# Hybrid decoder trunk on one core: scores of the first query block over its own keys alone, and the last two weight blocks of w_out taken together

## The chip, the cores and the metric

The kernel runs on one core of one Trainium2 chip. The metric is the time of one execution on the device in microseconds. The times are those of whole executions; the span of a profile runs from the first to the last instruction.

## What is computed

The reference is a decoder trunk of two layers over 512 tokens of width 1024. Each layer is cut here to what matters:

```python
h = rmsnorm(x, norm_mix)
z = h @ w_in                      # q, k, v of attention; q, k, v, gates of the mLSTM; branch gates
# branch A: attention of 128-query blocks over their own and the previous block
qb = q.reshape(B, nb, 128, 2, 4, 64)
prev = jnp.pad(tb, ((0, 0), (1, 0), (0, 0), (0, 0), (0, 0)))[:, :-1]   # block 0: zeros
scores = jnp.einsum('bnqhgd,bnkhd->bnhgqk', qb, kb) * 64 ** -0.5
valid = (kpos >= 0) & (kpos <= qpos) & (qpos - kpos < 128)
scores = jnp.where(valid, scores, -jnp.inf)                # softmax with a learned sink per head
# branch B: a chunkwise mLSTM
mixed = sigmoid(g_a) * (att @ w_att_branch) + sigmoid(g_m) * (hm @ w_m_branch)
x = x + mixed @ w_out
u = relu(rmsnorm(x, norm_ffn) @ w_ff1)
x = x + (u * u) @ w_ff2           # width 4096
```

For the first query block the previous block does not exist: its scores are masked whatever they are.

## The kernel before

All matrix products run in a split form: each float32 operand is written as a high part and a low rest, and three matmuls (high by high, low by high, high by low; the function `mm3`, recorded at L45) stand for one. A dense product goes through `group_steps`: four PSUM tiles of 128x512 take their sums side by side, one weight block (`chunk`) after the other. A block is loaded by DMA from SP's queue, its high part `wh` is made on ScalarE (L190) and its low part `wl` on VectorE (L191); `wh` and `wl` have four buffers, the raw block three. A step is one block by one tile, three matmuls. At the end of a group, `finish` empties the four tiles (`evac`). The PSUM tiles come in pairs of two banks from `banks()`, and three such pairs and two auxiliary tiles (`aux`) exist.

The input projection, the output projection and the MLP are such groups. `weave` runs the list of steps of a dense group and drops small steps of the attention and of the mLSTM between them: `k_tr(b)` transposes the keys of a block into `kT` (L505 and following: ScalarE L512 and L513, VectorE L514 and L515), `q_tr(b)` transposes queries (L534, L535), `att_scores(b, kv, hp)` multiplies queries and keys for two heads into one `aux` tile, `att_softmax(b, kv)` works on four heads at once (maximum L561 and L562, exponentials L567, the sink's L569, the sum and its reciprocal L570 and L571, product L572), and the gates of the mLSTM (L620 to L633) share the same engines. The order in which each engine gets its instructions is set by a tile scheduler that works from this program and from estimated durations; each engine then runs its list strictly in that order and waits where an operand is not there.

`kT` holds five blocks of 128 keys, a block of zeros ahead of the four real ones, so that every query block reads 256 columns: its own keys and the block before. The scores of a block end on VectorE in L554, a copy under the causal mask, which also releases the `aux` tile. For the blocks after the first, the previous keys' half is copied on ScalarE (L553); for block 0 that half is filled with a large negative number by GpSimd.

The output projection runs in two halves of 512 columns, j = 0 and 1, each with eight weight blocks. The adds of its result into the residual stream (L792) are `ev_x`. After it comes the MLP: its first matrix is loaded in pieces `f` (L856), its second in pieces `raw` (L924), both from SP's queue in program order, and both are split on ScalarE (L817) and VectorE (L818). The normalised input of the MLP is transposed on TensorE (L49), copied on ScalarE (L203) and VectorE (L204); the sums for the norm are taken at L283 and L311.

Of the kernel before, what the change touches and what calls it, by code (L numbers as in the profile page):

```python
# [16 lines left out]
P = 128  # L17
T = 512
# [15 lines left out]
def hybrid_kernel(ctx, tc, x, norm_mix, w_in, att_q_norm, att_k_norm, att_sinks, m_gate_bias,  # L34
# [3 lines left out]
    ve, sc, gp = nc.vector, nc.scalar, nc.gpsimd  # L38
# [21 lines left out]
    def nm(s):  # L60
        uid[0] += 1
        return f"{s}_{uid[0]}"
# [11 lines left out]
    def temp(dt=F32):  # L74
        return now["tmp"].tile([P, T], dt, tag="t", name=nm("t"))
# [3 lines left out]
    def banks(which=None):  # L79

        if which is None:
            which = "xyf"[turn_of[0] % 3]
            turn_of[0] += 1
        return psum.tile([P, 2, T], F32, tag=which, name=nm("mm"))

    def aux(shape=(P, T)):
        return paux.tile(list(shape), F32, tag="aux", name=nm("aux"))
# [4 lines left out]
    def f32(ap):  # L92
        return ap.bitcast(F32)
# [70 lines left out]
    def chunk(src, width=T):  # L164

        with tc.high_priority():
            raw = now["wraw"].tile([P, T], F32, tag="w", name=nm("w"))
            off = 0
            for s in src:
                n = s.shape[1]  # L170
                if first_loads:

                    n0 = {0: 0, 1: 2, 2: 4, 3: 6}.get(chunks[0], 7)
                    with tc.issue_after(first_loads[n0].ins):
                        nc.sync.dma_start(raw[:, off:off + n], s)
                    chunks[0] += 1
                    if chunks[0] == 8:
                        first_loads.clear()
                else:
                    nc.sync.dma_start(raw[:, off:off + n], s)  # L180
                off += n
            wh = now["wsp"].tile([P, T], F32R, tag="wh", name=nm("wh"))
            wl = now["wsp"].tile([P, T], F32R, tag="wl", name=nm("wl"))
            n = chunks[0] - 1 if first_loads else 2
            with ExitStack() as order:
                if n < 2:

                    order.enter_context(tc.issue_after(norm0.hi[n].ins))
                    order.enter_context(tc.issue_after(norm0.lo[n].ins))
                sc.activation(wh[:, :off], raw[:, :off], AF.Copy)  # L190
                ve.tensor_tensor(wl[:, :off], raw[:, :off], f32(wh[:, :off]), op=ALU.subtract)  # L191
        return wh, wl
# [14 lines left out]
    def mm3(ps, sh, sl, mh, ml, first, last, **kw):  # L207
        pe.matmul(ps, sh, mh, start=first, stop=False, **kw)
        pe.matmul(ps, sh, ml, start=False, stop=False, **kw)
        pe.matmul(ps, sl, mh, start=False, stop=last, **kw)  # L210

    def group_steps(acts, srcs, evac, width, mm, order=None):


        order = order or list(range(len(acts)))
        ps, w = [], []

        def step(k, m):
            if k == order[0] and m % 2 == 0:
                two = banks()  # L220
                ps.extend([two[:, 0, :], two[:, 1, :]])
            if m == 0:
                w[:] = chunk(srcs(k))
            mm(ps[m], slice(m * P, (m + 1) * P), w, acts[k], k == order[0], k == order[-1])

        def finish():
            with tc.high_priority():
                for m in range(4):
                    evac(m, ps[m][:, :width])

        return [(0.25, lambda k=k, m=m: step(k, m)) for k in order for m in range(4)] + [(0, finish)]

    def feat_steps(acts, srcs, evac):

        def mm(ps, c, w, a, first, last):
            mm3(ps, w[0][:, c], w[1][:, c], a[0], a[1], first, last)

        return group_steps(acts, srcs, evac, T, mm)

    def tok_steps(acts, srcs, evac, width=T, order=None):  # L240

        def mm(ps, c, w, a, first, last):
            mm3(ps[:, :width], a[0][:, c], a[1][:, c], w[0][:, :width], w[1][:, :width], first, last)

        return group_steps(acts, srcs, evac, width, mm, order)

    def weave(fill, side=()):

        side = sorted(side, key=lambda e: e[0])
        at = 0.0  # L250
        for width, f in fill:
            while side and side[0][0] <= at + 1e-6:
                side.pop(0)[1]()
            f()
            at += width
        for _, f in side:
            f()
# [97 lines left out]
    def mixer(l, norm, late, order, phase):  # L355
# [11 lines left out]
        acts = norm.acts  # L367
# [8 lines left out]
        def ev_kv(b, ps):  # L376
            sc.activation(kvi[:, b, :], ps, AF.Copy, scale=norm.col[:, b:b + 1])

        weave(tok_steps(acts, wcols(C_Q, 512), ev_q, order=order)
              + tok_steps(acts, lambda k: [W[k * P:(k + 1) * P, C_K:C_K + 256],  # L380
                                           W[k * P:(k + 1) * P, C_IF:C_IF + 8]], ev_kv, width=264),
              late + [(6.9, norm.columns), (10.0, lambda: row.append(norm.along()))])
# [89 lines left out]

        kT = mid.tile([P, 2, HKV, (NB + 1) * P], F32R, tag="mid10", name=nm("kT"))
        kTh, kTl = kT[:, 0], kT[:, 1]
        ve.memset(f32(kT[:, :, :, 0:P]), 0.0)

        v2 = mid.tile([P, NB, HKV, 2, HD], F32R, tag="mid4", name=nm("v2"))
        v4 = kvi[:, :, 128:256].rearrange("p b (h d) -> p b h d", d=HD)
# [59 lines left out]
        def att_scores(b, kv, hp):  # L538
            if hp == 0:
                sps[b, kv] = temp()  # L540
            ps = aux()
            for i in range(2):
                c = 2 * hp + i
                lhs = qT[b, kv][:, c * P:(c + 1) * P]
                o = ps[:, i * 2 * P:(i + 1) * 2 * P]
                pe.matmul(o, lhs, kTh[:, kv, b * P:(b + 2) * P], start=True, stop=False)
                pe.matmul(o, lhs, kTl[:, kv, b * P:(b + 2) * P], start=False, stop=True)
            p4 = ps.rearrange("p (h w k) -> p h w k", h=2, w=2)
            dst = sps[b, kv][:, hp * 2 * P:(hp + 1) * 2 * P].rearrange("p (h k) -> p h k", h=2)
            if b == 0:  # L550
                gp.memset(dst, NEG)
            else:
                sc.activation(dst, p4[:, :, 0, :], AF.Copy)  # L553
            ve.copy_predicated(dst, tri_i.unsqueeze(1).to_broadcast([P, 2, P]), p4[:, :, 1, :])  # L554
# [117 lines left out]
        for i, (b, kv) in enumerate(units):  # L672
            at = 7 + 1.65 * i
            side += [(at, lambda b=b, kv=kv: att_scores(b, kv, 0)),
                     (at + 1.25, lambda b=b, kv=kv: att_scores(b, kv, 1)),
                     (at + 1.25, lambda b=b, kv=kv: att_softmax(b, kv)),
                     (at + 3.45, lambda b=b, kv=kv: att_probs(b, kv)),
                     (at + 3.45 + 2.2, lambda b=b, kv=kv: att_out(b, kv))]
            if kv == 0 and b + 1 < NB:
                if b + 2 < NB:  # L680
                    side += [(at + 1, lambda b=b: k_vec(b + 2)), (at + 1, lambda b=b: q_vec(b + 2))]
                side += [(at + 2 * 1.65 - 1.25, lambda b=b: k_tr(b + 1)), (at + 2 * 1.65 - 1.75, lambda b=b: q_tr(b + 1))]
# [84 lines left out]
        def head_tr(f):  # L767
            ps = aux()
            for b in range(NB):
                pe.transpose(ps[:, b * P:(b + 1) * P], hm[b][:, f * P:(f + 1) * P], ident)  # L770
            hmT.append(split(ps, g_head(l, f)))

        side += [(57.75 + 1.25 * f, lambda f=f: head_tr(f)) for f in range(MH)]
        weave(feat_steps(acts, wcols(C_QM, 512), ev_qk) + s0 + s1 + tok_steps(acts, wcols(C_VM, 512), ev_v)
              + a_steps(0, g0) + a_steps(1, g1) + s2 + tok_steps(acts, wcols(C_OM, 512), ev_o) + s3, side)
        sgm = [g2, g3]
        mixed = [None] * KT
# [11 lines left out]
        for j in range(2):  # L789
            def ev_x(b, ps, j=j):  # L790
                xb = xtok[b // 2][j][:, b % 2, :]
                ve.tensor_tensor(xb, xb, ps, op=ALU.add)  # L792

            weave(tok_steps(mixed, lambda k, j=j: [w_out[l, k * P:(k + 1) * P, T * j:T * (j + 1)]], ev_x),
                  norm.steps(0, 1.5, 0.5) if j else [])
        return norm

# [228 lines left out]
    order = None  # L1026
    for l in range(DEPTH):
        with ExitStack() as phase:
            norm = mixer(l, norm, late, order, phase)
        late = norm.steps(1, 1.5, 0.5)  # L1030
        with ExitStack() as phase:
            norm = mlp(l, norm, late, phase)
        late = norm.steps(0, 1.5, 0.5) if norm else []
        order = [4, 5, 6, 7, 0, 1, 2, 3]
# [40 lines left out]
```

## Time and profile before

| | |
|---|---|
| times of three runs | 1333.98, 1333.02, 1332.83 us; median 1333.02 |
| profiled execution | 1333.96 us, span 1332.2 us |
| instructions | 16887 |
| TensorE (PE) | busy 98% of the span, 6106 matmuls |
| VectorE (DVE), ScalarE (ACT), GpSimd (POOL) | 70%, 50%, 8% |
| granted clock of TensorE | 1.000 |
| HBM | read 121.84 MB, written 2.10 MB, 93 GB/s over the span |

A row of the timeline has the start, the duration, the engine, the line, the operation, the tiles (output, then inputs), the shape and the count, and in brackets the idle time before it and what ended that. Where rows are grouped, the duration spans all of them. A matmul's end is modelled, so its price in a stream is the distance between starts. Layer 1 takes about the first half of the span and layer 2 the second.

### The profile page before, as it was taken

To read this page: it belongs to the slowest core of one execution; us is meant where nothing else is said; L and a number is where in the kernel's file an instruction comes from. 1 tells how busy PE (TensorE), PEld (TensorE's weight loads), DVE (VectorE), ACT (ScalarE), POOL (GpSimd) and SP (SyncE) were. 2 spreads that over 40 slices of the span, in tenths; PEclk is the share of its full clock that TensorE was granted. 3 is DMA by queue.
4 is the path that set the end of the run, shared out by engine and by line. 5 is a ranking of instruction groups with operands and counts; after the bars stand their busy time and mean duration, and the time that the engine had idled before them with its cause. 6 is when DMAs were issued, how large, how long until landed. Compare 5 with 4: busy or idle time off the path is not lost.

```text
span 1332.2 us, 16887 instructions
## 1 busy us (share of the span) xinstructions
PE 1311.5 (98%) x6106; PEld 1078.1 (81%) x6106; DVE 927.7 (70%) x1411; ACT 666.6 (50%) x1201; POOL 107.3 (8%) x215
## 2 busy tenths in 40 slices
PE   8999999999999999999999999999999999999998
PEld 6877788888788888888888777888887888888886
DVE  4689764473576876868947887654646778678687
ACT  5468765444434344343554787554334444344343
POOL 4512300000000000000015113000000000000000
PEclk9999999999999999999999999999999999999999
DMA  5322123421523243131024221243225232332211
GB/s 151 108 77 67 64 71 87 128 96 63 195 90 127 65 131 121 64 124 44 31 66 121 69 72 64 72 127 96 95 75 186 79 127 86 121 95 95 95 48 63
DMA packets 87282, 125.02 MB, mean 94 GB/s; under 512 B 8216, under 2 KB 45184, under 8 KB 87200
## 3 DMA queue, kind: packets, MB, share of 16 engines
q1 hardware_dynamic: 86240, 123.30, 29.5%
q8 instruction: 48, 0.79, 0.2%
q10 hardware_dynamic: 576, 0.53, 0.1%
q0 software_dynamic: 384, 0.13, 0.1%
q14 instruction: 34, 0.28, 0.1%
HBM read 121.84 MB, written 2.10 MB: 93 GB/s over the span
## 4 chain that ended last, share of the span: by engine, by line
PE 88%; DVE 6%; ACT 3%; issue 1%; DMA 1%; POOL 0%; ACTq 0%; SPq 0%; DVEq 0%; POOLq 0%
PE mm L45 82%; PE aux L45 4%; PE aux L49 2%; DVE wl L191 1%; ACT t L567 1%; ACT wh L190 1%; DVE t L554 1%; DMA w<-in_w_in_dram 0%; DVE t L604 0%; ACT wh L817 0%; DMA f<-in_w_ff_dram 0%; DVE t L201 0%; DVE t L535 0%; DVE wl L818 0%; ACT junk L283 0%
## 5 line engine op out<-in xcount | busy, mean ns | idle before, releaser
L45 PE MATMUL mm<-i,wh 128*128 128x512 f32 x1664 | 521.8, 393 | 2.3 <-DVE a L654 1.1
L45 PEld LDWEIGHTS mm<-i,wh 128*128 128x128 f32 x1664 | 307.4, 188 | 65.9 <-DVE a L654 2.0
L45 PE MATMUL mm<-i,wl 128*128 128x512 f32 x832 | 324.8, 390 | 0.0
L191 DVE TENSOR_TENSOR wl<-w,wh 128x512 fp32r<-128x512 f32 (+1 forms) x208 | 140.8, 678 | 125.8 <-ACT wh L190 120.6
L190 ACT ACTIVATE wh<-w 128x512 fp32r<-128x512 f32 (+1 forms) x208 | 127.2, 612 | 145.4 <-PE mm L45 122.5
L817 ACT ACTIVATE wh<-raw 128x1024 fp32r<-128x1024 f32 x112 | 118.2, 1055 | 151.9 <-PE mm L45 116.4
L45 PEld LDWEIGHTS mm<-i,wl 128*128 128x128 f32 x832 | 156.2, 188 | 33.2 <-issue 0.5
L45 PE MATMUL mm<-wh,uh 128*128 128x512 f32 x448 | 174.5, 389 | 0.0
L45 PE MATMUL mm<-wh,ul 128*128 128x512 f32 x448 | 174.3, 389 | 0.0
L45 PE MATMUL mm<-wl,uh 128*128 128x512 f32 x448 | 174.3, 389 | 0.0
L818 DVE TENSOR_TENSOR wl<-raw,wh 128x1024 fp32r<-128x1024 f32 x112 | 136.0, 1220 | 37.8 <-ACT wh L817 37.4
L45 PE MATMUL mm<-wh,i 128*128 128x512 f32 (+1 forms) x512 | 149.7, 370 | 0.4 <-ACT wh L190 0.4
L817 ACT ACTIVATE wh<-f 128x1024 fp32r<-128x1024 f32 x64 | 67.2, 1056 | 117.6 <-PE mm L45 87.9
L45 PEld LDWEIGHTS mm<-wh,i 128*128 128x128 f32 x512 | 92.4, 189 | 15.9 <-ACT wh L190 0.8
L45 PEld LDWEIGHTS mm<-wh,ul 128*128 128x128 f32 x448 | 84.1, 188 | 17.5
L45 PEld LDWEIGHTS mm<-wl,uh 128*128 128x128 f32 x448 | 84.1, 188 | 17.5
L45 PEld LDWEIGHTS mm<-wh,uh 128*128 128x128 f32 x448 | 84.1, 188 | 17.3
L818 DVE TENSOR_TENSOR wl<-f,wh 128x1024 fp32r<-128x1024 f32 x64 | 77.7, 1221 | 29.0 <-ACT wh L817 28.9
L45 PE MATMUL mm<-wl,i 128*128 128x512 f32 (+1 forms) x256 | 94.2, 368 | 0.0
L871 DVE SCALAR_TENSOR_TENSOR u<-mm,t 128x1024 f32<-128x1024 f32 x32 | 39.1, 1222 | 69.1 <-PE mm L45 69.1
L841 DVE TENSOR_TENSOR x<-x,mm 128x1024 f32<-128x1024 f32 x64 | 77.3, 1218 | 13.6 <-PE mm L45 13.6
L45 PE MATMUL mm<-wh,a 128*128 128x512 f32 x256 | 81.4, 393 | 0.0
(215 smaller groups left out, 1621.7 us busy)
## 6 DMA issues: line engine op xcount, KB each, us to landing
w<-in_w_in_dram SPq DMA_DIRECT2D x128, 256.0 KB, 2.6
f<-in_w_ff_dram SPq DMA_DIRECT2D x64, 512.0 KB, 3.7
raw<-in_w_ff_dram SPq DMA_DIRECT2D x64, 512.0 KB, 3.4
w<-in_w_out_dram SPq DMA_DIRECT2D x32, 256.0 KB, 2.5
w<-in_w_att_branch_dram SPq DMA_DIRECT2D x16, 256.0 KB, 2.5
w<-in_w_m_branch_dram SPq DMA_DIRECT2D x16, 256.0 KB, 2.5
w<-in_w_in_dram SPq DMA_DIRECT2D x16, 128.0 KB, 2.1
out_dram<-x SPq DMA_DIRECT2D x8, 256.0 KB, 2.2
```

The source lines that it names most:

```text
L45: return nc.tensor.matmul(*args, **kw)
L49: return nc.tensor.transpose(*args)
L190: sc.activation(wh[:, :off], raw[:, :off], AF.Copy)
L191: ve.tensor_tensor(wl[:, :off], raw[:, :off], f32(wh[:, :off]), op=ALU.subtract)
L554: ve.copy_predicated(dst, tri_i.unsqueeze(1).to_broadcast([P, 2, P]), p4[:, :, 1, :])
L567: sc.activation(s3[:, i, :], s3[:, i, :], AF.Exp, bias=m[:, i:i + 1], accum_out=den[:, i:i + 1])
L817: sc.activation(hi, r, AF.Copy)
L818: ve.tensor_tensor(lo, r, f32(hi), op=ALU.subtract)
L841: ve.tensor_tensor(xh, xh, ps, op=ALU.add)
L871: ve.scalar_tensor_tensor(dst, self.ps, 0.0, rowf[0].unsqueeze(1).to_broadcast([P, 2, T]), op0=ALU.max, op1=ALU.mult)
```

## The change

Two edits are made. In `att_scores`, block 0 multiplies its queries with its own 128 keys alone, into the right half of each 256 columns of the `aux` tile; the left half is neither written nor read. With this the zero block of `kT` is read by nobody, and the memset of it goes. In the second half of the output projection (j = 1), the steps of the last two weight blocks are ordered by tile: tile 0 with block 6, tile 0 with block 7, tile 1 with block 6, and so on, in place of block 6 for all tiles and then block 7. For this `w` becomes a dictionary by block.

```diff
-    def group_steps(acts, srcs, evac, width, mm, order=None):
+    def group_steps(acts, srcs, evac, width, mm, order=None, end_pair=False):
         order = order or list(range(len(acts)))
-        ps, w = [], []
+        n = len(order) - 2 if end_pair else len(order)
+        blocks = [[k] for k in order[:n]] + ([order[n:]] if end_pair else [])
+        ps, w = [], {}
 
         def step(k, m):
 ...
             if m == 0:
-                w[:] = chunk(srcs(k))
-            mm(ps[m], slice(m * P, (m + 1) * P), w, acts[k], k == order[0], k == order[-1])
+                w[k] = chunk(srcs(k))
+            mm(ps[m], slice(m * P, (m + 1) * P), w[k], acts[k], k == order[0], k == order[-1])
 ...
-        return [(0.25, lambda k=k, m=m: step(k, m)) for k in order for m in range(4)] + [(0, finish)]
+        return ([(0.25, lambda k=k, m=m: step(k, m)) for ks in blocks for m in range(4) for k in ks]
+                + [(0, finish)])
 ...
-        ve.memset(f32(kT[:, :, :, 0:P]), 0.0)
 ...
-                pe.matmul(o, lhs, kTh[:, kv, b * P:(b + 2) * P], start=True, stop=False)
-                pe.matmul(o, lhs, kTl[:, kv, b * P:(b + 2) * P], start=False, stop=True)
+                ks = slice(b * P, (b + 2) * P)
+                if b == 0:
+                    o, ks = o[:, P:], slice(P, 2 * P)
+                pe.matmul(o, lhs, kTh[:, kv, ks], start=True, stop=False)
+                pe.matmul(o, lhs, kTl[:, kv, ks], start=False, stop=True)
 ...
-            weave(tok_steps(mixed, lambda k, j=j: [w_out[l, k * P:(k + 1) * P, T * j:T * (j + 1)]], ev_x),
+            weave(tok_steps(mixed, lambda k, j=j: [w_out[l, k * P:(k + 1) * P, T * j:T * (j + 1)]], ev_x,
+                            end_pair=j == 1),
                   norm.steps(0, 1.5, 0.5) if j else [])
```

More of the change, by code (lines that the diff above doesn't have):

```diff
@@ L238, in feat_steps, with tok_steps @@
         return group_steps(acts, srcs, evac, T, mm)
-    def tok_steps(acts, srcs, evac, width=T, order=None):
+    def tok_steps(acts, srcs, evac, width=T, order=None, end_pair=False):
         def mm(ps, c, w, a, first, last):
             mm3(ps[:, :width], a[0][:, c], a[1][:, c], w[0][:, :width], w[1][:, :width], first, last)
-        return group_steps(acts, srcs, evac, width, mm, order)
+        return group_steps(acts, srcs, evac, width, mm, order, end_pair)
     def weave(fill, side=()):
```

## The prediction

> **What bounds the kernel now.** I read the page first, then TensorE's waits, then the timeline at the edited places.
>
> ```profile
> span 1332.2 us, 16887 instructions
> ...
> PE 1311.5 (98%) x6106; PEld 1078.1 (81%) x6106; DVE 927.7 (70%) x1411; ACT 666.6 (50%) x1201; POOL 107.3 (8%) x215
> ...
> PE 88%; DVE 6%; ACT 3%; issue 1%; DMA 1%; POOL 0%; ACTq 0%; SPq 0%; DVEq 0%; POOLq 0%
> ...
> PE aux L49 <- DVE t L554: 2.2, 6, 0.4
> ...
> PE aux L49 <- DVE x L792: 0.7, 2, 0.3
> PE mm L45 <- DVE x L792: 0.5, 2, 0.2
> ```
>
> TensorE is busy for 98% of the span; only 20.7 us of 1332.2 are not its own. So a matmul that goes is worth its issue time, and a wait that TensorE gains is paid in full, if nothing later swallows either. The last three rows (engine, line, what was waited for: us in total, times, longest) are the waits beside the two edits: on L554, the masked copy that empties a PSUM tile of scores, and on L792, the adds that end w_out.
>
> The sum is made against the profiled execution, 1333.96 us, of which 1332.2 are the span and 1.76 lie around it. It stands 0.94 above the median of the three runs, 1333.02, to which the difference is added.
>
> **Part 1, the scores of block 0.** Per layer, four groups of four score matmuls (kv 0 and 1, two halves each) go from 256 columns to 128: 16 matmuls, 32 in all. Their price now, and the nearest rows for 128 columns:
>
> ```profile
> 71.59 0.64 PE L45 MATMUL aux<-kT,t 128*128 128x256 f32 x4
> 72.06 0.40 PE L45 MATMUL mm<-i,wh 128*128 128x512 f32 x1
> ...
> 73.46 0.60 PE L49 MATMUL aux<-ident,a 128*128 128x128 f32 x4
> ...
> 187.11 0.33 PE L45 MATMUL aux<-a,a 128*128 128x128 f32 x2
> 187.28 0.68 PE L45 MATMUL mm<-a,wh 128*128 128x512 f32 x2
> ...
> L49 PE MATMUL aux<-ident,a x64: 270/272/303, 62.1 to 921.6; 128*128 128x128 f32 x64
> ```
>
> A group of 256 columns takes 72.06 - 71.59 = 0.47 us, 0.118 a matmul. Two of 128 columns take 187.28 - 187.11 = 0.17, so four take 0.34: that is the row of the same kind, and I take it. Transposes of 128 columns bound it from above: four span 0.60, one lasts 0.272, so they start (0.60 - 0.272) / 3 = 0.109 apart, 0.44 a group. Half of the present price, 0.235, bounds it from below. The saving is 0.13 a group (0.03 to 0.235), over 8 groups 1.04 us (0.24 to 1.9).
>
> That TensorE's price has a floor in the load of the 128 weight columns is a rule of the Trainium skill, page "TensorE: Matmul & The Clock Gate", section "LDWEIGHTS (loading the stationary operand)": P / 1.2 ns, 107 ns for 128 columns, with no term for the moving side. The transposes' 109 ns agree with it, the pair's 85 ns does not; by it the saving would be an estimated 8 x 4 x (118 - 107) ns = 0.35 us.
>
> **The memset** is one per layer on VectorE:
>
> ```profile
> L475 DVE MEMSET kT<- x2: 485/485/485, 1.0 to 671.6; 128x512 f32 x2
> ```
>
> It stands in the first microsecond of the program and at 671.6, before the keys exist. VectorE is idle for 30% of the span there and elsewhere, and the list of who waited for the memset is empty: 0 us. If it did delay something, at most 2 x 0.485 = 1 us would be gained.
>
> **What part 1 moves.** The order in which the program stands is rebuilt with shorter scores, and it comes out otherwise at one place, alike in both layers. On ScalarE, the split `wh` (L190, at 75.09) that stood before the four exponentials of the first softmax now stands after the second of them; and the split at 80.77, ahead of the two key copies L512 and L513, now stands between them. On TensorE the transpose of the second key block (`aux<-ident,kvi`) comes one dense matmul earlier, with the last use of a weight chunk behind it. On VectorE the small step of the maximum (L562) now stands behind a gate product (L633, 0.69) instead of a rotary product (L535, 0.48). The rest of VectorE's order at this place stays, as do the queues of SP and POOL. These are the rows of that place:
>
> ```profile
> 73.81 0.73 PE L45 MATMUL aux<-kT,t 128*128 128x256 f32 x4
> ...
> 74.72 0.48 DVE L535 SCALAR_TENSOR_TENSOR t<-aux,gc,t 64x256 fp32r<-64x256 f32 x1
> ...
> 75.09 0.63 ACT L190 ACTIVATE wh<-w 128x512 fp32r<-128x512 f32 x1 [0.52 <-PE mm L45]
> ...
> 75.22 0.17 DVE L562 SCALAR_TENSOR_TENSOR m<-m,nsinks 128x4 f32<-128x4 f32 x1
> ...
> 75.42 0.69 DVE L633 TENSOR_TENSOR a<-a,a 64x512 fp32r<-64x512 f32 x1
> ...
> 75.62 0.39 ACT L567 ACTIVATE t<-t,m 128x128 f32<-128x128 f32 x1
> ...
> 77.16 0.19 ACT L569 ACTIVATE es<-es 128x4 f32<-128x4 f32 x1
> ...
> 77.39 0.16 DVE L570 TENSOR_TENSOR den<-den,es 128x4 f32<-128x4 f32 x1 [0.48 <-ACT es L569]
> ...
> 77.79 0.69 DVE L572 TENSOR_TENSOR t<-t,den 128x512 f32<-128x512 f32 x1
> ...
> 80.27 0.44 DVE L554 COPY_PREDICATED t<-tri_l,aux 128x256 f32<-128x256 int32 x1
> ...
> 80.77 0.63 ACT L190 ACTIVATE wh<-w 128x512 fp32r<-128x512 f32 x1
> ...
> 80.86 0.30 PE L49 MATMUL aux<-ident,kvi 128*128 128x128 f32 x1 [0.42 <-DVE t L554]
> 80.91 0.47 PE L45 MATMUL mm<-i,wl 128*128 128x512 f32 x1
> ...
> 81.48 0.69 DVE L191 TENSOR_TENSOR wl<-w,wh 128x512 fp32r<-128x512 f32 x1 [0.22 <-ACT wh L190]
> ...
> 82.93 0.22 DVE L515 CAST kT<-kT 64x128 fp32r<-64x128 f32 x1
> ...
> 83.10 0.73 PE L45 MATMUL aux<-kT,t 128*128 128x256 f32 x4
> ...
> 739.53 0.30 PE L49 MATMUL aux<-ident,kvi 128*128 128x128 f32 x1 [0.43 <-DVE t L554]
> ```
>
> There are two auxiliary PSUM tiles. The third score group (73.81) holds one until L554 empties it at 80.27, because the whole softmax stands before that copy on VectorE. The key transpose needs that tile, and TensorE stands idle 0.42 us for it.
>
> Now the same chain in the new order. L562 is done at 75.22 + 0.17 + (0.69 - 0.48) = 75.60, and the exponentials start at about 75.65. Four of them take 77.16 - 75.62 = 1.54, the split among them 75.62 - 75.09 = 0.53: L569 starts at 77.72 in place of 77.16, 0.56 later. VectorE waits for L569 already (0.48 at 77.39), so L570, L572, the rotary products and L554, which follow almost without a gap, all come 0.56 later, and the transpose starts at 80.86 + 0.56 = 81.42. TensorE arrives there earlier than before, by the shorter groups and by the dense matmul that now comes later. All that it has saved in three groups it spends waiting.
>
> Second step. The split that began at 80.77, before the transpose, must now wait for the last use of the weight chunk, which stands behind it: 81.42 + 0.05 (the 80.86 and 80.91 rows) + 0.47 = 81.94, 1.17 later. Its `wl` on VectorE (81.48) stands ahead of L514 and L515, as before, so L515 ends 1.17 later than 82.93 + 0.22 = 83.15. The group at 83.10, the scores of block 1, reads what L515 writes. So TensorE is 1.17 late there, the fourth group's saving spent too, and up to 1.4 if the dense matmul that it still has to do (0.23) is counted. If L562 comes no later than it did, both are 0.21 less, 0.96 and 1.19. I take 1.25 a layer, **+2.5 us** in all (1.9 to 2.8). The 739.53 row shows layer 2 with the same wait. I see no later wait on something independent of TensorE's own progress that would swallow it.
>
> **Part 2, the end of w_out.** The last 24 matmuls of the second half are the same 24, taken tile by tile. They cost nothing new; the tiles' ends move.
>
> ```profile
> 334.52 3.62 SPq L924 DMA_DIRECT2D raw<-in_w_ff_dram  x3
> ...
> 335.89 2.66 DVE L792 TENSOR_TENSOR x<-x,mm 128x512 f32<-128x512 f32 x4 [8.14 <-PE mm L45]
> ...
> 336.37 0.39 PE L45 MATMUL mm<-wh,a 128*128 128x512 f32 x1
> ...
> 336.82 0.40 PE L45 MATMUL mm<-wh,a 128*128 128x512 f32 x1
> ...
> 338.00 0.44 PE L49 MATMUL aux<-ident,x 128*128 128x128 f32 x2 [0.34 <-DVE x L792]
> ...
> 337.00:340.00 3.00, 2.41 (x14) 1.65 (x13) 2.91 (x5) 0.45 (x1) 0.00 (x0) 1.00 0.59 203
> ...
> 348.93 1.05 ACT L817 ACTIVATE wh<-f 128x1024 fp32r<-128x1024 f32 x1
> ...
> 357.60 1.10 PE L45 MATMUL aux<-t,ones 128*128 128x512 f32 x2 [0.20 <-DVE t L311]
> ...
> 1007.02 0.69 ACT L203 ACTIVATE i<-aux,gcol 128x512 fp32r<-128x512 f32 x1 [1.14 <-PE aux L49]
> ```
>
> The adds wait by pairs of tiles. Those of the second pair wait for the last matmul of all (336.82 + 0.40 = 337.22) in both orders, and the third and fourth of the four 0.66 us adds set when the transposes at 338.00 and the MLP's first matmuls start. The first two come earlier, but VectorE had finished them by 335.89 + 2 x 0.66 = 337.2 anyhow. So the two L792 waits stay: 0. If they all went, 0.7 + 0.5 = 1.2 us would be gained; if one add were later, 2 x 0.66 lost.
>
> The price is in the loads. The first `raw` load of the MLP's second matrix is issued at 334.52, when the seventh weight block is released, twelve matmuls from the end. Now that block is used until three before the end; nine matmuls at (336.82 - 336.37) / 2 = 0.225 make this load 2.0 later. The next two keep their release (the eighth block's last use). Behind them on SP's queue stand the `f` loads. In 337 to 340 the DMA engines were busy for 0.59 of the time at 203 GB/s (the last two columns), so (1 - 0.59) x 3 = 1.23 us of slack takes that up and the stream is about 0.8 late. ScalarE's L817 at 348.93 starts on its `f` as soon as ScalarE is free; its load may have landed well before or just then: the split is 0 to 0.8 late, the norm behind it on ScalarE too, and the wait at 357.60 for that norm grows by as much. I take the middle, **+0.4 us**, in layer 1. In layer 2 ScalarE is idle for 1.14 us just before the same split (1007.02, the split follows at once), so its chain is not full there: 0 (up to 0.8).
>
> **Sum.** 2.5 + 0.4 = 2.9: 1333.96 + 2.9 = 1336.9 for a profiled execution like this one, 1333.02 + 2.9 = **1335.9 us** for the median. Of the 1.04 us of matmul time saved, none is seen.
>
> **Rivals.**
>
> B, the other side: the waits do not grow. If ScalarE's and VectorE's chains have more slack than I read, or TensorE's later waits shrink by what it lost, the shorter scores remain: 1333.02 - 1.04 = 1332.0. For it: TensorE is the bound, and what it does not issue is gained. Against: the 0.42 wait exists already, so anything put into the chain ahead of L554 is paid at once. It decides where L569 comes no later than now, for which the 0.53 of the split has to find a gap among the exponentials; the rows from 75.62 on show none.
>
> C, the weight load sets the price of a short matmul, as the transposes' 0.109 has it: with B's waits the saving is 8 x 4 x (0.118 - 0.109) = 0.3 us, 1332.7. For it are the 64 transposes; against it is the pair at 187.11. This is the rule of the Trainium skill named above.
>
> D, the MLP's weights become the bound: if the stream is late by a whole 0.5 MB load, at 203 GB/s 2.6 us, in place of 0.8, layer 1 loses 2.6 - 0.4 = 2.2 more than I count: 1338.1. It decides from where the delay at L817 passes the 0.8.
>
> E, the edit of the end of w_out brings the MLP forward, the L792 waits go: 1.2 off the forecast, 1334.7. For it is only that two of four tiles end earlier; against it, that the last pair decides.
>
> **How the numbers follow.** The forecast has 0.52, B 0.25, C 0.08, D 0.09, E 0.06. The range is 1331.9 to 1337.4: down to B; up to 2.8 for the attention and 1.6 for loads late by 0.8 in both layers. Left out are about half of B, whose saving may be up to 1.9, and most of D. About 0.2% (2.7 us) is what a measurement of this kernel tells from no change: beyond it on the fast side lies only B's end with E's, 0.06; beyond it on the slow side lie the upper part of the forecast, 0.35, and D, 0.09: 0.44; within it 0.50.
>
> **What would show it.** Right: score groups of block 0 that take about 0.34; the wait at the second key transpose grown from 0.42 to about 1.6 in both layers, L554 still its releaser, with TensorE some 1.2 later at the scores of block 1; the two L792 waits unchanged; the wait for L311 near 0.6 in layer 1. Wrong: L569 no later than before; that transpose starting no later; TensorE at the end of the attention part ahead of before.

## The result, and the profile after

The changed kernel takes 1337.28 us (median of eight runs, 1336.27 to 1338.82); the kernel before, run beside it, 1333.64 (eight runs, 1332.83 to 1333.98). The ratio is 1.0028, with a 95% interval of 1.0020 to 1.0037: slower by about 3.6 us. Forecast were 1335.9, in a range of 1331.9 to 1337.4.

The page of the profile after, and TensorE's waits (engine, line, what was waited for: us in total, times, longest). Lines after the edited places are shifted: L554 is now L561, L792 is L799, L311 is L315, L569 is L576, L514 and L515 are L517 and L518.

```profile
span 1335.6 us, 16885 instructions
...
PE 1312.4 (98%) x6106; PEld 1078.1 (81%) x6106; DVE 926.3 (69%) x1409; ACT 666.4 (50%) x1201; POOL 106.7 (8%) x215
```

```profile
PE aux L49 <- DVE t L561: 3.8, 6, 1.2
...
PE aux L45 <- DVE t L561: 1.0, 2, 0.5
...
PE aux L49 <- DVE x L799: 0.7, 2, 0.3
...
PE mm L45 <- DVE x L799: 0.5, 2, 0.3
```

The span is 3.4 us longer. TensorE's busy time has not fallen. The wait for the mask copy has grown from 2.2 to 3.8 us, a new wait on the same line, for the copy of another score group, has appeared with 1.0, and the two waits on the adds at the end of w_out are what they were: 0.7 and 0.5.

The timeline after, at the place where the prediction put the loss:

```profile
71.94 0.56 PE L45 MATMUL aux<-kT,t 128*128 128x128 f32 x4
...
76.76 0.62 ACT L190 ACTIVATE wh<-w 128x512 fp32r<-128x512 f32 x1
...
78.06 0.19 ACT L576 ACTIVATE es<-es 128x4 f32<-128x4 f32 x1
...
81.16 0.44 DVE L561 COPY_PREDICATED t<-tri_l,aux 128x256 f32<-128x256 int32 x1
...
81.75 0.30 PE L49 MATMUL aux<-ident,kvi 128*128 128x128 f32 x1 [1.24 <-DVE t L561]
...
82.36 0.63 ACT L190 ACTIVATE wh<-w 128x512 fp32r<-128x512 f32 x1
...
83.03 0.69 DVE L191 TENSOR_TENSOR wl<-w,wh 128x512 fp32r<-128x512 f32 x1 [0.87 <-ACT wh L190]
...
84.02 0.42 DVE L561 COPY_PREDICATED t<-tri_l,aux 128x256 f32<-128x256 int32 x1
...
84.47 0.22 DVE L518 CAST kT<-kT 64x128 fp32r<-64x128 f32 x1
...
84.59 0.78 PE L45 MATMUL aux<-kT,t 128*128 128x256 f32 x4 [0.48 <-DVE t L561]
...
741.90 0.30 PE L49 MATMUL aux<-ident,kvi 128*128 128x128 f32 x1 [1.24 <-DVE t L561]
```

This execution was 0.35 us late already at the second score group (71.94 against 71.59): about half of that it brings from its first 50 us, and the rest it loses at the start of the first score group (68.01 against 67.62). Why is open. Without the 0.35, the sink's exponential is 0.55 later than before, the mask copy and the transpose 0.54, the end of the keys' low part 1.19, and the scores of block 1 start 1.14 later. The wait at the transpose is 1.24 in place of 0.42, in both layers, and a second wait of 0.48 stands at the scores of block 1.

### The profile page after: what moved, and what is told of

It reads as the page before. It is cut to its first block, busy times and chain, and to the rows that moved or that the text cites. A ratio compares the mean times of both kernels' runs of the same rounds, so it can differ in the third digit from the quotient of the medians.

```text
span 1335.6 us, 16885 instructions
## 1 busy us (share of the span) xinstructions
PE 1312.4 (98%) x6106; PEld 1078.1 (81%) x6106; DVE 926.3 (69%) x1409; ACT 666.4 (50%) x1201; POOL 106.7 (8%) x215
## 4 chain that ended last, share of the span: by engine, by line
PE 88%; DVE 6%; ACT 4%; issue 1%; DMA 1%; POOL 0%; ACTq 0%; SPq 0%; DVEq 0%; POOLq 0%
PE mm L45 82%; PE aux L45 4%; PE aux L49 2%; ACT t L574 1%; DVE wl L191 1%; ACT wh L190 1%; DVE t L561 1%; DVE t L611 0%; DMA w<-in_w_in_dram 0%; DVE t L201 0%; ACT wh L825 0%; DVE t L538 0%; ACT junk L287 0%; DVE t L579 0%; DMA grow<-in_norm_mix_dram 0%
```

## The experiments

Two traces with the same matmuls can be compared matmul by matmul: the start of the k-th one in this trace less its start in the trace of before is how late TensorE is there. What that grows by in a stretch is what the stretch costs, whatever came earlier. The stretches are attention 1 (63.7 to 131.3 us of before), MLP 1 (338.0 to 519.8) and attention 2 (711.2 to 795.8). In the table, "old" is the order of before and "new" that of the changed kernel; medians are in us, and each ratio is against the runs of before on the same chip (median 1333.64 for the changed kernel, 1334.06 to 1334.37 for the others). low_half has a single run and no ratio. Each stretch is that of one profiled execution. The diffs below show the lines that matter, in short form.

| kernel | order | block 0, columns | end of w_out | median | ratio (95%) | attention 1 | MLP 1 | attention 2 |
|---|---|---|---|---|---|---|---|---|
| changed kernel | new | 128 | by tile | 1337.28 | 1.0028 (1.0020 to 1.0037) | +1.77 | -0.01 | +1.51 |
| part2_only | old | 256 | by tile | 1333.69 | 0.9999 (0.9990 to 1.0007) | +0.05 | +0.36 | +0.11 |
| part1_only | new | 128 | as before | 1337.18 | 1.0024 (1.0015 to 1.0033) | +1.70 | +0.01 | +1.75 |
| old_order_short | old | 128 | by tile | 1333.95 | 1.0001 (0.9992 to 1.0010) | -0.05 | +0.45 | -0.04 |
| new_order_full | new | 256 | by tile | 1337.17 | 1.0024 (1.0013 to 1.0034) | +1.59 | -0.02 | +1.78 |
| short_alone | old | 128 | as before | 1333.80 | 0.9996 (0.9987 to 1.0005) | -0.01 | 0.00 | -0.05 |
| step1_undone | first place old | 128 | by tile | 1336.07 | 1.0017 (1.0008 to 1.0026) | +1.04 | +0.86 | +1.81 |
| step2_undone | second place old | 128 | by tile | 1335.14 | 1.0006 (0.9997 to 1.0015) | +0.59 | +0.56 | +0.67 |
| early_mask | three pins | 128 | by tile | 1337.51 | 1.0023 (1.0014 to 1.0033) | +2.10 | +0.03 | +2.06 |
| mask_earlier | old, mask copy up | 128 | as before | 1334.59 | 1.0004 (0.9995 to 1.0013) | +0.45 | +0.02 | +0.24 |
| low_half | new | 128 and 64 | by tile | 1336.92 | (one run) | +1.63 | +0.19 | +1.69 |
| f_first | old, f loads up | 128 | by tile | 1346.42 | 1.0096 (1.0079 to 1.0113) | +0.11 | +6.19 | -0.05 |

**The order and the width apart.** Four kernels. The first two do one part each. The other two are built twice: the first build gives the order of each engine, the second gets that order and the other width.

```diff
 part2_only: scores and memset of before
-                if b == 0:
 ...
-                    o, ks = o[:, P:], slice(P, 2 * P)
 ...
+        ve.memset(f32(kT[:, :, :, 0:P]), 0.0)
 part1_only: end of w_out of before
-                            end_pair=j == 1),
 old_order_short and new_order_full (the other way round)
+    _, _, order = build(False)             # 256 columns: the order of before
+    nc, arrays, _ = build(True, order)     # 128 columns, every queue chained in that order
```

> Only the end of w_out is ordered by tile; scores and memset are those of before, and so is every engine's order elsewhere. Theory O (all of the loss comes from the order at the second key transpose): the time of before, 1333.6 us, within 0.4; the two waits on the x adds 0.6 us a layer as before, the wait for the norm at 357.6 us stays 0.20. Theory L (the later raw load costs): 1334.0 to 1335.2, with that wait at 0.6 or more.

> Only the scores of block 0 are shortened and the memset left out; w_out is as before. Theory O: the time of the whole change, 1337.3 us, within 0.4, with the wait at the second key transpose 1.2 us in both layers. Theory L: lower than the whole change by what the loads cost, 1335.7 to 1336.9.

> Both parts of the change, the memset kept, but every engine is given its instructions in the order of before. Theory O: 1333.0 to 1333.6 us: the chain to the second key transpose is that of before, the wait there is 0.42 plus the 0.24 us that TensorE saves in three groups, and the rest of the 0.64 us saved may come through. Theory W (the short groups are the cause, whatever the order: TensorE runs ahead and waits longer for everything behind it): 1336 to 1337.3.

> The counterpart: 256 columns again for block 0, with the memset, but every engine in the order of the changed kernel. Theory O: the time of the changed kernel, 1337.3 us, within 0.5, since VectorE's and ScalarE's chain sets the transpose; TensorE reaches it 0.24 us later and waits about 1.0 in place of 1.24. Theory W: near before, 1333.6 to 1334.5.

Their waits between 78 and 86 us; first old_order_short, then new_order_full:

```profile
PE aux L61 <- DVE t L574: 0.4, 1, 0.4
```

```profile
PE aux L61 <- DVE t L574: 1.2, 1, 1.2
PE aux L57 <- DVE t L574: 0.4, 1, 0.4
```

The order alone makes the loss: with it the kernel is slow at either width, and without it, at neither. The width alone brings nothing that can be seen in the times. Theory O's sizes of the wait were wrong, though: 0.4 and not 0.66 in old_order_short, 1.19 and not 1.0 in new_order_full. It took the chain on VectorE for fixed, while the chain starts from the score groups and came earlier with TensorE; and it took three groups to save 0.24, which is too much (see the price of a short matmul). part2_only is at the time of before, as theory O has it, but its trace shows theory L's wait:

```profile
PE aux L45 <- DVE t L315: 0.6, 1, 0.6
```

**The two steps.** The order of the changed kernel differs from that of before at two places. Each was put back alone.

```diff
 step1_undone: ScalarE's queue up to the sink's exponential, and VectorE's, from the old order
+    order[act] = old[act][:cut1] + new[act][cut1:mid] + old[act][mid:cut2] + new[act][cut2:]
+    order[dve] = old[dve]
 step2_undone: ScalarE's queue behind the sink's exponential, and TensorE's, from the old order
+    order[act] = new[act][:cut1] + old[act][cut1:mid] + new[act][mid:cut2] + old[act][cut2:]
+    order[pe] = old[pe]
```

> The changed kernel, memset kept, with the first place alone put back: ScalarE's split stands ahead of the four exponentials again and VectorE has the order of before; the second place (the transpose one dense matmul earlier, the split between the two key copies) stays as in the changed kernel. Theory two steps: the sink's exponential and the mask copy come back by 0.6 us a layer and the second step's 1.0 us a layer stays: before plus 2.0, some 1335.8 us, wait at the transpose near 0.7 to 0.9. Rival, the first place alone is the cause: the time of before, 1333.6 to 1334.1. Rival, the second alone: 1337.2.

> The counterpart: the split between the exponentials stays as in the changed kernel, the second place is put back (the split ahead of both key copies, TensorE's order of before). Theory two steps: the transpose starts 0.6 us late in each layer, the key copies no later than that: before plus 1.2, some 1335.0 us, wait at the transpose about 1.0. Rival, the first place alone: 1337.2. Rival, the second alone: 1333.6 to 1334.1.

The timelines of step1_undone, then of step2_undone:

```profile
81.63 0.30 PE L62 MATMUL aux<-ident,kvi 128*128 128x128 f32 x1 [0.64 <-DVE t L575]
...
84.47 0.78 PE L58 MATMUL aux<-kT,t 128*128 128x256 f32 x4 [0.47 <-DVE t L575]
```

```profile
81.34 0.30 PE L62 MATMUL aux<-ident,kvi 128*128 128x128 f32 x1 [1.02 <-DVE t L575]
...
83.56 0.76 PE L58 MATMUL aux<-kT,t 128*128 128x256 f32 x4
```

The two steps are there, and in attention 1 they add up: the second step costs 1.04 alone and the first 0.59, together 1.63, against 1.59 to 1.77 with both. With the first step undone the wait at the transpose is down to 0.64 and the one at the scores of block 1 stays; with the second undone it is the other way round. In attention 2, step1_undone gained nothing (+1.81), which the two steps do not explain: 0.78 of it came before the transpose, 0.6 of that at the third score group, where TensorE waits 0.39. Why is open. From 737 us of before on, it loses 1.03, and step2_undone 0.79, together 1.82 against 1.62 to 1.82 with both. The times are too coarse for the sum: the medians are 1.7 and 0.8 above before, together 2.5 against 3.1 in part1_only and new_order_full, with intervals of some 1.2 to either side. The profiled execution of step1_undone is also its slowest, 1338.42 against the median of 1336.07.

**Freeing the PSUM tile earlier.** Two tries to get the short scores' saving.

```diff
 early_mask: pins on the changed kernel; the rest of the order is rebuilt
+    pins = [("first rotary product", "maximum's small step"), ("wh", "exp 1 to 4"), ("second wh", "first key copy")]
 mask_earlier: short_alone, and on VectorE
+        order[dve].insert(at - 2, mask)    # ahead of the weight split and a rotary product
```

> The changed kernel with three places pinned: the first softmax's exponentials behind the split that stood ahead of them before, the maximum's small step behind the first rotary product, the first key copy behind its split. With these the rebuilt order also puts the mask copy of the third score group ahead of the softmax's product, and the key transpose nine dense matmuls earlier. Theory O with two PSUM tiles as the limit: the wait at the transpose (0.42 a layer before) goes and the saving of 0.64 comes through: before minus 0.8 to 1.5 us, 1332.2 to 1333.2. Rival: the wait moves to the key copies or the next score group, and the time is that of before, 1333.6 to 1334.1.

> The short scores alone, in the order of before, memset kept, the end of w_out as before. Theory O: nothing of the 0.64 us is seen in the time, 0 to 0.3 below before: the three groups' saving goes into the wait at the second key transpose (0.42 to 0.66), the fourth's into the wait for the key's low part at the scores of block 1. The wait for the norm in the MLP of layer 1, 0.58 and 0.67 where the end of w_out was re-ordered in the old order, is 0.20 again. Rival: the saving comes through, before minus 0.6.

> As the one before, and on VectorE the mask copy of the third score group (the one that frees the PSUM tile) moved up by two instructions, ahead of a weight split and a rotary product. Theory two limits: the wait at the transpose goes (0.66 a layer), but the key's low part behind it still ends at its own time, set by the weight split on ScalarE, so some 0.24 us a layer are gained: before minus 0.3 to 0.8. Rival, the tile is the only limit: before minus 1.3. Rival, the delayed weight split makes TensorE wait: above before.

Timelines of early_mask and of mask_earlier:

```profile
79.14 0.44 DVE L578 COPY_PREDICATED t<-tri_l,aux 128x256 f32<-128x256 int32 x1
...
79.73 0.30 PE L49 MATMUL aux<-ident,kvi 128*128 128x128 f32 x1 [1.37 <-DVE t L578]
...
84.47 0.79 PE L45 MATMUL aux<-kT,t 128*128 128x256 f32 x4 [0.53 <-DVE t L578]
```

```profile
79.36 0.27 PE L62 MATMUL aux<-ident,kvi 128*128 128x128 f32 x1
...
80.69 0.66 PE L58 MATMUL aux<-kT,t 128*128 128x128 f32 x4 [0.59 <-DVE t L552]
```

early_mask failed: the pins put a query copy and the split ahead of the exponentials, so the mask copy came only 1.1 us earlier (79.14 against 80.27), while the transpose now stood nine matmuls earlier and waited 1.37. mask_earlier did take the wait at the transpose away, and TensorE then waits 0.59 for the other PSUM tile, which the rotary product frees that was delayed for it. Here, what one tile gets earlier the other gets later. short_alone shows how little of the saving is left at the end of the two stretches: 0.01 and 0.05 us. No kernel here beats the one before by more than the noise.

**The price of a short matmul.**

```diff
 low_half: the matmul with the low part of the keys, in block 0
+                if b == 0:
+                    o, ks = o[:, :OWN[0]], slice(P, P + OWN[0])     # OWN[0] is 64
                 pe.matmul(o, lhs, kTl[:, kv, ks], start=False, stop=True)
```

> The order of the changed kernel, and in block 0 the matmul with the low part of the keys takes 64 of its 128 columns (it leaves out half of the low part's share). Price theory F (the load of 128 weight columns sets a short matmul's price, about 0.11 us): a group of four stays at 0.39 to 0.40 us. Theory S (the columns that stream set it): 0.33 to 0.35 us. The time: that of the changed kernel, 1336.5 to 1338, as the group's saving would be waited away.

The second score group and the dense matmuls behind it, in the kernel before, the changed kernel and low_half:

```profile
71.59 0.64 PE L45 MATMUL aux<-kT,t 128*128 128x256 f32 x4
72.06 0.63 PE L45 MATMUL mm<-i,wh 128*128 128x512 f32 x2
72.53 0.39 PE L45 MATMUL mm<-i,wl 128*128 128x512 f32 x1
```

```profile
71.94 0.56 PE L45 MATMUL aux<-kT,t 128*128 128x128 f32 x4
72.33 0.68 PE L45 MATMUL mm<-i,wh 128*128 128x512 f32 x2
72.85 0.39 PE L45 MATMUL mm<-i,wl 128*128 128x512 f32 x1
```

```profile
71.09 0.53 PE L57 MATMUL aux<-kT,t 128*128 128x128 f32 x4
71.45 0.71 PE L57 MATMUL mm<-i,wh 128*128 128x512 f32 x2
72.00 0.39 PE L57 MATMUL mm<-i,wl 128*128 128x512 f32 x1
```

Up to the dense matmul behind it the group takes 0.47, 0.39 and 0.36 us; the 0.36 lies between the two expectations. But what is short there comes back one matmul later. The single starts of these traces give four steps in the group and a fifth, from the first dense matmul to the second:

| kernel | steps in the group | fifth step | sum |
|---|---|---|---|
| before | 0.116, 0.120, 0.119, 0.118 | 0.232 | 0.705 |
| changed kernel | 0.059, 0.113, 0.109, 0.113 | 0.283 | 0.677 |
| low_half | 0.058, 0.081, 0.143, 0.080 | 0.315 | 0.677 |

Elsewhere dense matmuls start some 0.23 apart. So a short group saves 0.03 us, not 0.08, some 0.24 in all eight. Without 0.227 for the dense matmul, four short ones take 0.45, 0.112 each. Half as many columns in every second matmul change nothing of that: theory F's price holds, though the group itself did not stay at 0.39. Whether it is the load of the weights or another fixed cost of a matmul, these runs do not tell apart.

**The loads behind the re-ordered end.**

```diff
 f_first: old_order_short, and on SP's queue, in each layer
+        for n in [the fourth and fifth load of f]:
+            order[sp].insert(order[sp].index(first raw load), n)
```

> Both parts in the order of before, as old_order_short, and on SP's queue the fourth and fifth load of the MLP's first matrix moved ahead of the first three loads of its second. What the re-ordered end of w_out makes late, the raw loads, then stands behind the f loads and cannot delay them. Theory L (the late raw load pushes the f loads, and through ScalarE the norm): between the 300 and 400 us of layer 1 TensorE loses nothing against before, where old_order_short lost 0.45; the wait for the norm is 0.2 or less; the time is before minus 0.1 to 0.5. Rival, the loss there has another cause: 0.4 stays. Rival, the raw loads themselves come too late for the second matrix: above before by 1 or more, with a wait at a split of raw.

Timelines of f_first, of SP's queue, ScalarE and TensorE:

```profile
339.81 1.66 SPq L883 DMA_DIRECT2D f<-in_w_ff_dram  x2
341.51 3.90 SPq L952 DMA_DIRECT2D raw<-in_w_ff_dram  x5
345.51 15.43 SPq L883 DMA_DIRECT2D f<-in_w_ff_dram  x5
...
356.67 1.06 ACT L844 ACTIVATE wh<-f 128x1024 fp32r<-128x1024 f32 x1 [4.51 <-DMA f<-in_w_ff_dram]
...
362.27 2.05 PE L58 MATMUL aux<-t,ones 128*128 128x512 f32 x2 [4.81 <-DVE t L328]
```

No expectation of f_first held: the time is above before, as in the second rival, but by 12 us, and the wait is at a split of f, not of raw. It shows the mechanism of theory L all the same. The raw loads, the first of which goes out at 334.52 before, now had to follow the two f loads and began at 341.51. The sixth f load stood behind all five of them; ScalarE waited 4.51 us for it, the norm behind it was late, and the wait at the norm rose to 4.81. Raw loads that go out late ahead of an f load are paid at that wait. That a later raw load alone does it in the re-ordered kernels is not tried by itself: it rests on their rows. In old_order_short the three raw loads go out together at 337.23, and the split that did not wait before (348.93) now waits for its load:

```profile
350.03 1.06 ACT L838 ACTIVATE wh<-f 128x1024 fp32r<-128x1024 f32 x1 [0.35 <-DMA f<-in_w_ff_dram]
```

## Why the prediction was right or wrong

- **The first step, 0.56 us later, held:** 0.55 at the sink's exponential, 0.54 at the transpose; step2_undone has it alone, 0.59.
- **The second step, 1.17 later, held:** 1.19 at the end of the keys' low part; step1_undone has it alone in attention 1, 1.04. The releaser was another: the scores of block 1 wait (0.48) for L561 at 84.02, the mask copy of the fourth score group, which frees their tile; their first matmul starts at 84.59, before L518 ends at 84.69. The copy and L518 stand behind the same late weight split on VectorE (83.03), so the delay is the one forecast.
- **The sum for the attention was too small:** 2.5 (1.9 to 2.8) against 1.77 + 1.51 = 3.3, and 3.4 to 3.5 in part1_only and new_order_full. The mis-sized term is TensorE's lateness for a given delay of the key's low part: I took 1.25 of a possible 1.4 a layer, and it was 1.5 to 1.8. Of the 1.77, 1.14 is the late start at 84.59 and 0.23 the dense matmul still to do; some 0.2 more appear between 85 and 90 us, behind which I saw no further loss, and their cause is open. Another 0.17 came ahead of the place, at the first score group.
- **The price of a group failed, at the step "two take 0.17, so four take 0.34".** Up to the dense matmul behind, it is 72.33 - 71.94 = 0.39; with what that matmul gives back, four take 0.45. The pair at 187.11 has the same shape: the two dense matmuls behind it, grouped at 187.28, span 0.68 instead of 0.63, and the next one starts at 187.80, so that the pair costs 0.23, 0.113 a matmul. So 0.03 a group is saved, 0.24 in all, and not 1.04; the transposes' 0.109, taken as the upper bound, was the price. The Trainium skill, page "TensorE: Matmul & The Clock Gate", section "LDWEIGHTS (loading the stationary operand)", puts the load of 128 columns at 107 ns; the trace agrees with its 112 ns a matmul. That the load is a floor of the price is a step of the prediction's own. Rival C had the price, a saving of 0.3, but not the time.
- **That none of the saving is seen held, but not for the reason given.** There was little to see, and it is not all spent at the transpose: short_alone has gained 0.09 us ahead of it in layer 1, and still has it at 86 us, behind the scores of block 1; then it goes in small amounts, and 0.01 is left at the end of the stretch, 0.05 in layer 2. The chain there moves with TensorE, so the wait stays 0.4.
- **The wait at the transpose was forecast at about 1.6 and is 1.24**: 0.30 of the difference is the saving of three groups, which was 0.09 and not 0.39.
- **The adds at the end of w_out: 0, held.** The waits are 0.7 and 0.5 in every kernel with and without the re-ordered end.
- **The loads, +0.4 in layer 1:** in the profiled execution of the changed kernel it is 0. Its first raw load is 2.0 later, as forecast (338.50 against 334.52, with TensorE 1.9 late), but the stream behind is not: the fifth f load lands 7.85 us after its issue, as before, and the wait for the norm is 0.20. But with the same end of w_out, part2_only shows 0.36, old_order_short 0.45, step2_undone 0.56, step1_undone 0.86, low_half 0.19, new_order_full 0; early_mask has 0.03 there and 0.41 in layer 2. The kernels without it show 0.00 to 0.02. So the term is there in some executions, and where it is, of about the size forecast. It goes with how fast the loads land: that f load takes 8.35 to 8.85 us in the four that lose 0.36 or more, 8.17 in low_half and 7.69 to 8.01 where nothing is lost. Why it lands sooner in one execution than in another is open. The times cannot show the term: part2_only's interval is 0.9990 to 1.0007.
- **The memset: 0.** new_order_full has it, the changed kernel has not; between 520 and 711 us, where the second one stands, TensorE's lateness changes by 0.03 us in both.

The difference came out near the forecast, 3.4 between the traces against 2.9, because a term that was too small (the attention, short by 0.8) and one that the changed kernel's trace did not show (the loads, 0.4) stood against each other. The medians differ by 3.6. The median after is 1.4 us above the forecast: 0.7 of that is the difference, and 0.6 the kernel before, 1333.64 over eight runs and 1333.02 over the three that the sum started from. It lies 0.12 below the top of the range, and that top holds 1.6 for late loads, of which this trace shows nothing: without them it would be 1335.8. That the range holds is luck in part; the direction and the two steps are not.

## What to carry to other kernels

A cheaper instruction is an input to the scheduler. Before counting its saving, compare the order of every engine: here two moves of a weight split, each by an instruction or two, cost 3.3 us where the change itself could save 0.24. Price a group of short matmuls up to the second dense matmul behind it, not the first. Where TensorE waits at a chain of other engines, see whether the chain starts from TensorE's own work: then it moves along, and the wait stays. And with two buffers, moving the release of one forward can hold up the other.

## What the runs showed of the hardware

After the 4.81 us without work in f_first, TensorE ran at about half its clock for over 3 us; the third column from the right, 0.54 and 0.61, is the granted clock.

```profile
357.00:362.00 5.00, 0.47 (x3) 0.04 (x1) 4.01 (x12) 2.70 (x6) 0.00 (x0) 1.00 0.43 131
362.00:364.00 2.00, 1.73 (x3) 0.84 (x3) 0.13 (x1) 0.00 (x0) 0.00 (x0) 0.54 0.74 198
364.00:366.00 2.00, 2.00 (x7) 1.52 (x6) 0.00 (x0) 0.60 (x1) 0.00 (x0) 0.61 0.21 73
366.00:368.00 2.00, 2.00 (x10) 1.64 (x9) 0.00 (x0) 0.01 (x1) 0.00 (x0) 1.00 0.00 0
```

From the first to the last matmul of that stretch TensorE falls behind by another 1.5 us. The Trainium skill has this in the page "TensorE: Matmul & The Clock Gate", section "What's actually happening": half clock after an idle window of about 3.4 us; the trace agrees. The waits of 1.24 us in the changed kernel did not do it: the clock granted from 79 to 88 us of its trace is 1.00.

A matmul of 256 columns costs 0.12 us in the groups above, one of 128 columns 0.112, and one of 512 columns 0.23. So here halving 512 columns halves the price, and halving 256 saves almost nothing.

The first 64 us, the same work in all these kernels, take between 1.60 us less and 0.85 us more than in the profiled execution of before. This is as large as most effects studied here, and why the stretches of the table start after it.
